# First three products of layer 0 of a two-layer attention model: advanced together over the arriving tiles of x

## The chip, the cores and the metric

The program runs on 1 core of one Trainium2 chip. The metric is device time in microseconds (us) of that core, given as the median of several runs of the whole program. The engines are PE (TensorE: matmuls and transposes), DVE (VectorE), ACT (ScalarE), POOL (GpSimd) and SP (SyncE, which here only issues DMAs). Each engine executes its instructions in the order of the program, and waits on semaphores for the others.

## The reference

The reference is a transformer of two layers over one sequence of 512 tokens of width 1024, in f32. Layer 0 mixes two kinds of attention heads. Eight "fox" heads have a decay from a forget gate. Eight "DSA" heads attend, per query, to the 128 keys that a small indexer scores highest, over a key-value latent of rank 128. Layer 1 has sixteen heads of block attention. Each layer ends with a gated feed-forward part with a short convolution. Cut to the part that the change touches:

```python
def rmsnorm(x, g):
    y = x * lax.rsqrt(jnp.mean(x * x, axis=-1, keepdims=True) + EPS) * g
...
    for layer in range(DEPTH):
        h = rmsnorm(x, attn_norm[layer])
        if layer % 2 == 0:
            proj = h @ w_in_even[i]
            fq, fk, fv, ff, dq, ckv, dkr, iq, ik, iw = jnp.split(proj, split_points, axis=-1)
            log_f = jax.nn.log_sigmoid(ff + b_fox_f[i])
            fox_out = fox_attention(fq, fk, fv, log_f)
            c_kv = rmsnorm(ckv, g_ckv[i])
            iq = apply_partial_rope(iq, cos, sin)
            ik = apply_partial_rope(ik, cos, sin)
            o_lat = dsa_attention(q_lat, q_rope, c_kv, k_rope, iq, ik, iw, dsa_topk)   # top 128 keys per query
            x = x + mixed @ w_out_even[i]
        else:
            ...
        x = x + conv_glu_ffn(rmsnorm(x, ffn_norm[layer]), ...)
    return rmsnorm(x, final_norm)
```

## The kernel before, in words

Everything is held transposed: x is eight tiles xT[0] to xT[7] of 128 features by 512 tokens. The factor 1/rms of a token does not depend on the feature, so the products start from x times g, and the factor is multiplied onto their results when they leave PSUM (RB, CR and SR hold it, spread over 128 partitions).

**Products.** An f32 product is made of three matmuls of a reduced-precision type. Each operand is split into a high part (a cast) and a low part (the rest): xh and xl of x, wh and wl of the weights. `mm3` adds high times high (line 154), high times low (155) and low times high (156). `proj` runs a product over the eight feature tiles: 24 matmuls of 512 columns, 5 to 6 us at full rate. `prep` makes xh on ACT (line 169) and xl on DVE (170) for one tile of x.

**Weights.** They come in chunks of 128 by 1024. `chunk` loads one by SP into a buffer "raw", ACT casts it to "wh", and DVE subtracts to get "wl"; once the flag lo_on_pool is set, from the fox heads' weights on, POOL subtracts instead (145 to 147). There are three buffers of each kind (N_W). SP goes through its loads in order, and a load waits until the raw buffer of three chunks ago is free.

**PSUM.** There are four pools of banks of 512 columns: "mm" with 3 for products, "S" with 2 for scores, "T" with 2 for transposes, "O" with 1 for the output of a head.

**The start, lines 479 to 552.** SP loads x tile 0, the first half of the chunk misc, x tile 1, the second half, the other x tiles, then iq0, iq1 and ckv whole. misc holds the small outputs (the indexer's key and weights, the rotary key, the forget gates), iq0 and iq1 the indexer's queries, ckv the latent. Product misc runs while x arrives. Squares of x go to ACT and are added into acc (the first three on POOL, 181) and acc2 (DVE, 499); DVE adds the two (500). `rope_angles` is a chain of tiny DVE operations for the rotary angles, and `rope_tables` transposes them on PE (tabT, 314). `rstd_main` then makes the factor 1/rms: PE transposes acc (st_n, 187), DVE sums it and takes the inverse root by Newton steps on four columns (194 to 196), PE transposes that back while spreading it (bc_n, 199), ACT copies it to RB. `rope` (217 to 221) takes a product from PSUM with CR and SR, one of its multiplications on POOL; `scaled` (226) takes one with RB.

**The heads, from line 585 on.** Eight head pairs of layer 0, four fox and four DSA, each with its key and query products (fk, fq), a value product (fv) for two pairs, the score blocks s_f in pool "S", their softmax (335 to 337), and the product with the values. `index_scores` (526) and `select` (543) are put between them by a work list: the indexer's scores go into tmask1 to tmask3, and sixteen rounds of MAX and MATCH_REPLACE on DVE find the top 128 per query; line 550 turns the result into a mask, which the first DSA head needs.

**What sets the order.** The code above only declares dependencies and an order of writing. A scheduler in the framework places the instructions of every engine into one fixed row per engine, by estimates of its own, and puts in the waits. So an edit at the start can move instructions on an engine far behind it.

## Time and profile before

| | before |
|---|---|
| median of 3 runs | 1278.89 us (1277.62 to 1280.02) |
| profiled execution, its own time | 1276.6 us |
| its span in the profile | 1274.8 us |
| granted clock of PE, mean | 0.994 of 2.4 GHz |
| PE busy | 1224.2 us, 96% |
| DVE busy | 845.7 us, 66% |
| ACT busy | 591.7 us, 46% |
| POOL busy | 311.0 us, 24% |

The times of single instructions below come from the profiled execution. A share of busy time is a mean over the whole span; stages differ. A busy PE counts a matmul from its start to its modelled end, and matmuls overlap.

### The profile page before, as it was taken

The numbers are of one execution on the slowest core, as the hardware profiler recorded it, in microseconds if no ns is written. First come the engines' busy times: TensorE is split into PE (matmuls) and PEld (weight loads), VectorE is DVE, ScalarE is ACT, GpSimd is POOL, SyncE is SP. The second block draws the span as 40 slices with busy tenths as digits, with TensorE's granted clock in tenths as the row PEclk, the third lists the DMA queues.
The fourth block names the chain that finished last, engine by engine and source line by source line (L and its number), as shares of the span: only waits on it lengthen the run. The fifth ranks groups of instructions, "written<-read, shape, count | busy, mean of one in ns | idle before, by whom it ended". The sixth has DMA issues, their size and how long they took to land.

```text
span 1274.8 us, 17004 instructions
## 1 busy us (share of the span) xinstructions
PE 1224.2 (96%) x6148; PEld 1024.0 (80%) x6148; DVE 845.7 (66%) x1629; ACT 591.7 (46%) x1011; POOL 311.0 (24%) x354
## 2 busy tenths in 40 slices
PE   6899989999999999999999999999999999999996
PEld 4778767778888888888888788778788888888896
DVE  7899998776555345554467879787755533665564
ACT  5585667654333123333336556556433321333443
POOL 3586656541110001110114323222111100111000
PEclk9999999999999999999999999999999999999998
DMA  5223222222333233333323232222233333223363
GB/s 191 67 77 106 76 59 73 61 73 93 99 99 99 92 91 99 99 100 99 100 90 93 85 97 68 82 83 67 83 100 99 99 99 98 88 97 99 118 189 107
DMA packets 37379, 120.95 MB, mean 95 GB/s; under 512 B 4736, under 2 KB 4864, under 8 KB 37296
## 3 DMA queue, kind: packets, MB, share of 16 engines
q1 hardware_dynamic: 36368, 118.51, 30.4%
q10 hardware_dynamic: 864, 1.17, 0.3%
q8 instruction: 48, 0.79, 0.3%
q14 instruction: 35, 0.29, 0.1%
q0 software_dynamic: 64, 0.20, 0.0%
HBM read 109.37 MB, written 2.10 MB: 87 GB/s over the span
## 4 chain that ended last, share of the span: by engine, by line
PE 79%; DVE 14%; ACT 3%; issue 3%; POOL 0%; DMA 0%; DVEq 0%; ACTq 0%; POOLq 0%
PE mm_d L155 6%; PE mm_d L154 6%; PE mm_d L156 6%; PE mm_u L156 6%; PE mm_u L155 6%; PE mm_u L154 6%; PE mm_g L155 6%; PE mm_g L154 6%; PE mm_g L156 6%; DVE tmask L548 1%; DVE xl L170 1%; PE o_m L367 1%; DVE m L547 1%; PE t_m L358 1%; PE o_m L368 1%
## 5 line engine op out<-in xcount | busy, mean ns | idle before, releaser
L422 POOL TENSOR_TENSOR cv<-cv,sg 128x512 f32<-128x512 f32 x44 | 56.9, 1293 | 543.0 <-ACT sg L421 543.0
L155 PE MATMUL mm_d<-a_l,wh_d 128*128 128x512 f32 (+1 forms) x440 | 152.7, 347 | 0.0
L156 PE MATMUL mm_d<-a_h,wl_d 128*128 128x512 f32 (+1 forms) x440 | 152.5, 347 | 0.0
L154 PE MATMUL mm_d<-a_h,wh_d 128*128 128x512 f32 (+1 forms) x440 | 152.5, 347 | 0.0
L155 PE MATMUL mm_g<-xl,wh_g 128*128 128x512 f32 x352 | 137.1, 390 | 0.0
L156 PE MATMUL mm_u<-xh,wl_u 128*128 128x512 f32 x352 | 137.1, 390 | 0.0
L154 PE MATMUL mm_g<-xh,wh_g 128*128 128x512 f32 x352 | 136.9, 389 | 0.0
L154 PE MATMUL mm_u<-xh,wh_u 128*128 128x512 f32 x352 | 136.9, 389 | 0.0
L155 PE MATMUL mm_u<-xl,wh_u 128*128 128x512 f32 x352 | 136.9, 389 | 0.0
L156 PE MATMUL mm_g<-xh,wl_g 128*128 128x512 f32 x352 | 136.9, 389 | 0.0
L143 ACT CAST wh_d<-raw_d 128x1024 fp32r<-128x1024 f32 x55 | 57.8, 1050 | 122.4 <-PE mm_d L155 83.5
L149 DVE TENSOR_TENSOR wl_d<-raw_d,wh_d 128x1024 fp32r<-128x1024 f32 x55 | 67.6, 1229 | 66.7 <-ACT wh_d L143 66.5
L143 ACT CAST wh_u<-raw_u 128x1024 fp32r<-128x1024 f32 x44 | 46.4, 1054 | 131.6 <-PE mm_g L155 114.6
L154 PEld LDWEIGHTS mm_d<-a_h,wh_d 128*128 128x128 f32 x440 | 83.3, 189 | 10.4
L156 PEld LDWEIGHTS mm_d<-a_h,wl_d 128*128 128x128 f32 x440 | 83.3, 189 | 10.3
L155 PEld LDWEIGHTS mm_d<-a_l,wh_d 128*128 128x128 f32 x440 | 83.3, 189 | 10.2
L417 DVE TENSOR_TENSOR gs<-mm_g,RB 128x512 f32<-128x512 f32 x44 | 30.4, 692 | 90.7 <-PE mm_g L156 90.2
L424 DVE TENSOR_TENSOR us<-mm_u,RB 128x512 f32<-128x512 f32 x44 | 30.4, 692 | 81.2 <-PE mm_u L156 81.2
L154 PEld LDWEIGHTS mm_g<-xh,wh_g 128*128 128x128 f32 x352 | 66.1, 188 | 13.8
L154 PEld LDWEIGHTS mm_u<-xh,wh_u 128*128 128x128 f32 x352 | 66.1, 188 | 13.8
L155 PEld LDWEIGHTS mm_u<-xl,wh_u 128*128 128x128 f32 x352 | 66.1, 188 | 13.7
L156 PEld LDWEIGHTS mm_g<-xh,wl_g 128*128 128x128 f32 x352 | 66.1, 188 | 13.6
(775 smaller groups left out, 3080.2 us busy)
## 6 DMA issues: line engine op xcount, KB each, us to landing
raw_d<-in_w SPq DMA_DIRECT2D x55, 512.0 KB, 3.5
raw_g<-in_w SPq DMA_DIRECT2D x44, 512.0 KB, 3.5
raw_u<-in_w SPq DMA_DIRECT2D x44, 512.0 KB, 3.5
raw_oe<-in_w SPq DMA_DIRECT2D x8, 512.0 KB, 3.5
raw_mv<-in_w SPq DMA_DIRECT2D x8, 512.0 KB, 3.6
raw_mk<-in_w SPq DMA_DIRECT2D x8, 512.0 KB, 3.6
raw_mq<-in_w SPq DMA_DIRECT2D x8, 512.0 KB, 3.6
raw_oo<-in_w SPq DMA_DIRECT2D x8, 512.0 KB, 3.5
```

The source lines that it names most:

```text
L143: A.copy(wh, raw)
L149: V.tensor_tensor(wl, raw, wh.bitcast(F32), op=OP.subtract)
L154: PE.matmul(out, ah, bh, start=first, stop=False)
L155: PE.matmul(out, ah, bl, start=False, stop=False)
L156: PE.matmul(out, al, bh, start=False, stop=last)
L170: V.scalar_tensor_tensor(xl[:, d], xT[:, d], gc, xh[:, d].bitcast(F32), op0=OP.mult, op1=OP.subtract)
L358: PE.transpose(t[:, n * P:n * P + P], probs[i][:, j * P:j * P + P], ident)
L367: PE.matmul(o[:, o0:o0 + w], vj, ph[:, c0:c0 + w], start=j == 0, stop=False)
L368: PE.matmul(o[:, o0:o0 + w], vj, pl[:, c0:c0 + w], start=False, stop=j == NB - 1)
L417: V.tensor_tensor(gs, og, RB, op=OP.mult)
L422: G.tensor_tensor(cv, cv, sg, op=OP.mult)
L424: V.tensor_tensor(us, ou, RB, op=OP.mult)
```

## The change

`chunk` loses its form with a cut, and `proj` the form that takes weights already loaded. A new function, `first_products`, takes the three chunks misc, iq0 and iq1, and an order of arrivals. Each step loads one x tile and preps it, or loads one half of a chunk (512 columns) and splits it on ACT and DVE. After every step it writes all the matmuls of the three products that have become possible: those of the x tiles so far against the halves so far. The three results stand in PSUM pools "O" (misc) and "S" (iq0, iq1) where they stood in "mm". The square of an x tile is written right behind its step, and `rope_angles` behind the fourth x tile.

Product ckv is now written right after the three, ahead of the last sum into acc, `rope_tables` and `rstd_main`; it stood behind the rotary work on misc and iq. The copy into cmask is written after the three products.

```diff
--- before.py
+++ after.py
@@ -128,17 +128,13 @@
 
     lo_on_pool = False
 
-    def chunk(name, cut=0):
-        raw = wp.tile([P, 1024], F32, tag="raw", bufs=N_W, name=f"raw_{name}")
-        wh = wp.tile([P, 1024], F32R, tag="wh", bufs=N_W, name=f"wh_{name}")
-        wl = wp.tile([P, 1024], F32R, tag="wl", bufs=N_W, name=f"wl_{name}")
-        if cut:
-            for s in (slice(0, cut), slice(cut, 1024)):
-                nc.sync.dma_start(raw[:, s], w_d[idx[name]][:, s])
-                split(wh[:, s], wl[:, s], raw[:, s])
-                if s.start == 0:
-                    nc.sync.dma_start(xT[:, 1], xT_d[:, 1])
-            return wh, wl
+    def w_tiles(name):
+        return (wp.tile([P, 1024], F32, tag="raw", bufs=N_W, name=f"raw_{name}"),
+                wp.tile([P, 1024], F32R, tag="wh", bufs=N_W, name=f"wh_{name}"),
+                wp.tile([P, 1024], F32R, tag="wl", bufs=N_W, name=f"wl_{name}"))
+
+    def chunk(name):
+        raw, wh, wl = w_tiles(name)
         nc.sync.dma_start(raw, w_d[idx[name]])
         A.copy(wh, raw)
         if lo_on_pool:
@@ -155,8 +151,8 @@
         PE.matmul(out, ah, bl, start=False, stop=False)
         PE.matmul(out, al, bh, start=False, stop=last)
 
-    def proj(name, w=None):
-        wh, wl = w or chunk(name)
+    def proj(name):
+        wh, wl = chunk(name)
         o = ps("mm", f"mm_{name}")
         for k in range(KT):
             s = slice(k * P, k * P + P)
@@ -477,19 +473,11 @@
 
 
     acc = sq_acc(0)
-    nc.sync.dma_start(xT[:, 0], xT_d[:, 0])
-    w = chunk("misc", 512)
-    for d in range(2, KT):
-        nc.sync.dma_start(xT[:, d], xT_d[:, d])
     nc.gpsimd.dma_start(const, const_d)
-    G.tensor_copy(cmask[:, 384:], const[:, C_TRI:C_TRI + P])
-    cs = rope_angles()
-    for d in range(KT):
-        prep(d, 0, None)
-    pmisc = proj("misc", w)
-    w = [chunk("iq0")]
     acc2 = tmp("acc2")
-    for d in range(KT):
+    angles = []
+
+    def first_square(d):
         if d < 4:
             square(d, acc)
         else:
@@ -497,12 +485,46 @@
             A.activation(s, xT[:, d], AF.Square)
             if d > 4:
                 V.tensor_tensor(acc2, acc2, s, op=OP.add)
+
+    def first_products(names, order):
+
+        w = {n: w_tiles(n) for n in names}
+        o = {n: ps(tag, f"mm_{n}") for n, tag in names.items()}
+        done = {n: 0 for n in names}
+        xs, halves_of = 0, {n: 0 for n in names}
+        for what in order:
+            if what == "x":
+                nc.sync.dma_start(xT[:, xs], xT_d[:, xs])
+                prep(xs, 0, None)
+                xs += 1
+            else:
+                h = halves_of[what]
+                s = slice(512 * h, 512 * h + 512)
+                raw, wh, wl = w[what]
+                nc.sync.dma_start(raw[:, s], w_d[idx[what]][:, s])
+                split(wh[:, s], wl[:, s], raw[:, s])
+                halves_of[what] += 1
+            for n in names:
+                while done[n] < min(xs, 4 * halves_of[n]):
+                    k = done[n]
+                    s = slice(k * P, k * P + P)
+                    mm3(o[n], w[n][1][:, s], w[n][2][:, s], xh[:, k], xl[:, k], k == 0, k == KT - 1)
+                    done[n] += 1
+            if what == "x":
+                first_square(xs - 1)
+                if xs == 4:
+                    angles.append(rope_angles())
+        return [o[n] for n in names]
+
+    pmisc, *piq = first_products({"misc": "O", "iq0": "S", "iq1": "S"}, [
+        "x", "misc", "x", "iq0", "x", "iq1", "x", "x", "misc", "x", "iq0", "x", "iq1", "x"])
+    G.tensor_copy(cmask[:, 384:], const[:, C_TRI:C_TRI + P])
+    pckv = proj("ckv")
     V.tensor_tensor(acc, acc, acc2, op=OP.add)
-    w.append(chunk("iq1"))
     V.tensor_copy(selr[0:96, :P], const[0:96, C_SEL:C_SEL + P])
     V.tensor_copy(selr[96:128, :P], const[64:96, C_SEL:C_SEL + P])
     V.tensor_scalar(selr[:, P:], const[:, C_FSEL:C_FSEL + 8], 0.5, None, op0=OP.mult)
-    rope_tables(cs)
+    rope_tables(angles[0])
     rcol = rstd_main(acc, "n0")
     rope_scaled()
 
@@ -520,7 +542,7 @@
     for b in range(NB):
         PE.transpose(t[:, b * P:b * P + P], ym[:, b * P:b * P + P], ident)
     A.activation(iwT, t.rearrange("p (b c) -> p b c", b=NB)[:, :, 104:108], AF.Copy, scale=0.0625)
-    iq = [stack_q(rope(proj(f"iq{h}", w[h]), f"iq{h}"), f"iq{h}") for h in range(2)]
+    iq = [stack_q(rope(piq[h], f"iq{h}"), f"iq{h}") for h in range(2)]
 
 
     def index_scores(i):
@@ -549,7 +571,7 @@
         if rounds.stop == TOPK // 8:
             V.tensor_scalar(sc, sc, -2e38, NEG, op0=OP.is_gt, op1=OP.mult)
 
-    y = scaled(proj("ckv"), "ckv")
+    y = scaled(pckv, "ckv")
     sq = tmp("sqkv")
     A.activation(sq, y, AF.Square)
     _, bc = rstd_of(sq, P, "kv")
```

What the scheduler makes of it is shown at three places. The numbers at the names' ends count tiles and differ between the two programs.

First PE, at the boundary of the first products: mm_misc and mm_iq are the results, xh and xl the parts of x, wh and wl those of the weights. Before, the last three matmuls of misc, and the first three of iq0:

```order
L154 MATMUL mm_misc<-xh,wh_misc 128x512
L155 MATMUL mm_misc<-xl,wh_misc 128x512
L156 MATMUL mm_misc<-xh,wl_misc 128x512
L154 MATMUL mm_iq_313<-xh,wh_iq_198 128x512
L155 MATMUL mm_iq_313<-xl,wh_iq_198 128x512
L156 MATMUL mm_iq_313<-xh,wl_iq_199 128x512
```

Now, nine matmuls on one tile of x, three for each product:

```order
L150 MATMUL mm_misc<-xh,wh_misc 128x512
L151 MATMUL mm_misc<-xl,wh_misc 128x512
L152 MATMUL mm_misc<-xh,wl_misc 128x512
L150 MATMUL mm_iq_113<-xh,wh_iq_107 128x512
L151 MATMUL mm_iq_113<-xl,wh_iq_107 128x512
L152 MATMUL mm_iq_113<-xh,wl_iq_108 128x512
L150 MATMUL mm_iq_114<-xh,wh_iq_110 128x512
L151 MATMUL mm_iq_114<-xl,wh_iq_110 128x512
L152 MATMUL mm_iq_114<-xh,wl_iq_111 128x512
```

The products of iq0 (mm_iq_113) and iq1 (mm_iq_114) stand among those of misc, where they stood behind all of them.

Next PE around st_n, the transposes of acc from which the norm's factor is made. Before, it stood within iq0's product:

```order
L314 MATMUL tabT<-const,exp_tab 128x128 x8
L154 MATMUL mm_iq_313<-xh,wh_iq_198 128x512
L187 MATMUL st_n_258<-const,acc_100 128x128 x4
L155 MATMUL mm_iq_313<-xl,wh_iq_198 128x512
L156 MATMUL mm_iq_313<-xh,wl_iq_199 128x512
L154 MATMUL mm_iq_350<-xh,wh_iq_226 128x512
```

Now, at the end of ckv's product and within that of fv, the first value product of the fox heads:

```order
L152 MATMUL mm_ckv<-xh,wl_ckv 128x512
L310 MATMUL tabT<-const,exp_tab 128x128 x5
L150 MATMUL mm_fv__0_483<-wh_fv_0_486,xh 128x256
L151 MATMUL mm_fv__0_483<-wl_fv_0_487,xh 128x256
L152 MATMUL mm_fv__0_483<-wh_fv_0_486,xl 128x256
L150 MATMUL mm_fv__0_483<-wh_fv_0_486,xh 128x256
L151 MATMUL mm_fv__0_483<-wl_fv_0_487,xh 128x256
L152 MATMUL mm_fv__0_483<-wh_fv_0_486,xl 128x256
L150 MATMUL mm_fv__1_484<-wh_fv_0_486,xh 128x256
L183 MATMUL st_n_345<-const,acc_100 128x128 x4
L151 MATMUL mm_fv__1_484<-wl_fv_0_487,xh 128x256
```

In PE's row st_n moved from behind 46 product matmuls to behind 72, the 24 of ckv and 7 of fv.

Last DVE, in the softmax of the second fox head: prt_f and mx_f are the numerator and maximum of a score block, sm_f a sum; the MAX and MATCH_REPLACE on tmask are a round of the selection. Before:

```order
L335 ISA prt_f_861,mx_f_0_866<-s_f_0_862,cmask 128x128
L335 ISA mx_f_0_866 128x1
L548 MATCH_REPLACE tmask_89<-m_1_1354,tmask_89 128x256
L335 ISA prt_f_861,mx_f_1_876<-s_f_1_872,cmask 128x256
L335 ISA mx_f_1_876 128x1
L547 MAX m_1_1357<-tmask_89 128x8
L337 RECIPROCAL sm_f_0_867<-sm_f_0_867 128x1
L548 MATCH_REPLACE tmask_89<-m_1_1357,tmask_89 128x256
L335 ISA prt_f_861,mx_f_2_886<-s_f_2_882,cmask 128x384
L335 ISA mx_f_2_886 128x1
L337 RECIPROCAL sm_f_1_877<-sm_f_1_877 128x1
L547 MAX m_1_1360<-tmask_89 128x8
```

Now:

```order
L331 ISA prt_f_867,mx_f_0_872<-s_f_0_868,cmask 128x128
L331 ISA mx_f_0_872 128x1
L569 MAX m_1_1351<-tmask_89 128x8
L331 ISA prt_f_867,mx_f_1_882<-s_f_1_878,cmask 128x256
L331 ISA mx_f_1_882 128x1
L333 RECIPROCAL sm_f_3_814<-sm_f_3_814 128x1
L333 RECIPROCAL sm_f_0_873<-sm_f_0_873 128x1
L570 MATCH_REPLACE tmask_89<-m_1_1351,tmask_89 128x256
L331 ISA prt_f_867,mx_f_2_892<-s_f_2_888,cmask 128x384
L331 ISA mx_f_2_892 128x1
L237 TENSOR_TENSOR fq_a<-sc_fq_942,fq_a 64x512
L333 RECIPROCAL sm_f_1_883<-sm_f_1_883 128x1
```

Fewer rounds stand between the blocks, and the query work of the second pair (fq_a) stands among them.

## Rows read from the trace of the kernel before

**Rows 1.** The page, first part: busy us, share of the span, instructions.

```profile
PE 1224.2 (96%) x6148; PEld 1024.0 (80%) x6148; DVE 845.7 (66%) x1629; ACT 591.7 (46%) x1011; POOL 311.0 (24%) x354
```

**Rows 2.** Windows: stretch, us, busy of PE PEld DVE ACT POOL, PEclk, DMA, GB/s.

```profile
60.00:200.00 140.00, 130.38 (x706) 106.34 (x704) 131.75 (x377) 93.83 (x209) 93.96 (x120) 1.00 0.27 74
67.00:184.00 117.00, 109.87 (x596) 89.76 (x596) 111.24 (x324) 76.58 (x168) 79.92 (x102) 1.00 0.29 81
...
220.00:280.00 60.00, 59.57 (x294) 48.19 (x294) 45.62 (x98) 36.59 (x77) 33.54 (x40) 1.00 0.25 71
```

**Rows 3.** Timeline of PE: start, us, line, out<-in, shape, count [idle before <-releaser].

```profile
14.60 0.79 PE L155 MATMUL mm_misc<-xl,wh_misc 128*128 128x512 f32 x1 [2.54 <-DVE xl L170]
...
19.45 0.39 PE L154 MATMUL mm_misc<-xh,wh_misc 128*128 128x512 f32 x1
19.68 0.40 PE L155 MATMUL mm_misc<-xl,wh_misc 128*128 128x512 f32 x1
...
25.59 1.03 PE L314 MATMUL tabT<-const,exp_tab 128*128 128x128 f32 x8
...
26.86 0.66 PE L187 MATMUL st_n<-const,acc 128*128 128x128 f32 x4
...
32.70 0.73 PE L199 MATMUL bc_n<-const,y_n 128*128 128x128 f32 x4 [2.20 <-DVE y_n L196]
...
33.66 0.63 PE L154 MATMUL mm_iq<-xh,wh_iq 128*128 128x512 f32 x1
34.08 0.63 PE L155 MATMUL mm_iq<-xl,wh_iq 128*128 128x512 f32 x1
...
37.71 0.39 PE L154 MATMUL mm_ckv<-xh,wh_ckv 128*128 128x512 f32 x1
...
43.76 0.28 PE L155 MATMUL mm_fv__0_477<-wl_fv,xh 128*128 128x256 f32 x1
43.88 0.28 PE L156 MATMUL mm_fv__0_477<-wh_fv,xl 128*128 128x256 f32 x1
```

**Rows 4.** DVE's waits from 60 to 210 us: total, times, longest.

```profile
DVE ry_dq L221 <- POOL rs_dq L220: 1.7, 2, 1.5
```

**Rows 5.** Timeline of PE, where the DSA heads' products begin.

```profile
203.07 0.50 PE L623 MATMUL mm_dk<-kr,selr 128*128 128x512 f32 x1 [1.48 <-DVE ry_dq L219]
```

**Rows 6.** Timeline of DVE: first and last of the selection's masks.

```profile
67.11 0.48 DVE L538 SCALAR_TENSOR_TENSOR tmask<-rl,iwT,cmask 128x256 f32<-128x256 f32 x1
...
177.07 0.67 DVE L547 MAX8 m<-tmask 128x8 f32<-128x512 f32 x1
...
180.77 0.73 DVE L550 TENSOR_SCALAR tmask<-tmask 128x512 f32<-128x512 f32 x1
```

**Rows 7.** Windows, during the first loads (columns as in rows 2).

```profile
4.00:12.00 8.00, 4.03 (x7) 1.88 (x7) 5.88 (x17) 6.74 (x12) 3.19 (x3) 1.00 1.03 376
```

**Rows 8.** Tiles, at the start: ns min/median/max, first and last start.

```profile
L169 ACT ACTIVATE xh<-xT,vec x8: 707/708/722, 5.3 to 12.7; 128x512 fp32r<-128x512 f32 x8
...
L170 DVE SCALAR_TENSOR_TENSOR xl<-xT,vec,xh x8: 740/742/751, 6.5 to 18.0; 128x512 fp32r<-128x512 f32 x8
...
L127 DVE TENSOR_TENSOR wl_misc<-raw_misc,wh_misc x2: 676/684/692, 7.8 to 11.9; 128x512 fp32r<-128x512 f32 x2
```

**Rows 9.** Timeline of DVE at the start, around acc.

```profile
8.38 1.25 DVE L270 TENSOR_SCALAR ang_n<-ang_r 128x32 f32<-128x32 f32 x1
...
24.09 0.69 DVE L500 TENSOR_TENSOR acc<-acc,acc 128x512 f32<-128x512 f32 x1
```

**Rows 10.** Timeline of DVE, beside POOL's split of weights and away from it.

```profile
29.10 0.61 DVE L195 TENSOR_TENSOR h_n<-h_n,ms_n 128x4 f32<-128x4 f32 x1
...
32.00 0.16 DVE L194 SCALAR_TENSOR_TENSOR h_n<-y_n 128x4 f32<-128x4 f32 x1
...
36.85 1.77 DVE L221 TENSOR_TENSOR ry_misc<-ry_misc,rs_misc 128x512 f32<-128x512 f32 x1 [0.21 <-POOL rs_misc L220]
...
46.92 0.69 DVE L221 TENSOR_TENSOR ry_iq<-ry_iq,rs_iq 128x512 f32<-128x512 f32 x1
```

## The prediction, made before the changed kernel ran

> **What bounds the kernel now.** The first line of the page says that PE is busy for 1224.2 of 1274.8 us [rows 1], but that is a sum over stages with different limits. The change sits in the first 45 us, so I read that stage and the one that it feeds. Between 60 and 200 us, the attention heads of layer 0, DVE is busy for 131.75 of 140 us and PE for 130.38 [rows 2]. The two look equal. They are not: a 128x512 matmul at full rate shows 0.39 us of busy time, while the next one starts 0.23 us after it [rows 3], so short gaps on PE are hidden under the tail of the matmul before, and DVE's operations leave no such tail. The waits say the same. DVE's longest cause of waiting in this stage is 1.7 us in all, for a product of POOL [rows 4]. PE, at 203.07 us, stands 1.48 us until DVE has emptied a PSUM tile [rows 5]. After that PE has little idle time: 59.57 of 60 us are busy from 220 to 280 us [rows 2]. So what the start of the kernel is worth is read at DVE: DVE sets when PE comes through at about 203 us, and from there on the time is PE's.
>
> DVE in this stage does two things: the work of the heads, and the rounds of the top-128 selection (MAX and MATCH_REPLACE on tmask1 to tmask3), which fill its gaps. The last mask is done at 180.77 us [rows 6], and the first DSA head needs it. Rounds that are put off must be made up before that point.
>
> **The loads.** SP issues fourteen loads of 256 KB at the start (eight of x, six half chunks), where it issued ten of 256 KB and two of 512. The bytes are the same, and nothing else is queued on SP until a buffer of weights comes free. From 4 to 12 us the queues moved 376 GB/s [rows 7], and nearly all that was on its way was loads of 256 KB. The last x tile now has the 1.05 MB of iq0 and iq1 ahead of it: 2.8 us at that rate. DVE, as shown next, comes to it at about 22 us, some 7 us after it lands. Price nothing; 2.8 us on the last nine matmuls if that cover were gone.
>
> **The splits.** ACT makes the eight xh from 5.3 us on, 0.71 us each [rows 8]; with eight squares and six half casts that is 22 operations, about 0.6 us each with their overlap: some 13 us, to about 18. DVE is later. Its last xl began at 18.0 us and took 0.74 [rows 8]. The new order puts four half splits (0.68 us each [rows 8], some 0.6 apart), two sums of squares like them and four tiny operations ahead of that one, so it ends at about 22.8. Each of POOL's three additions to acc holds DVE for a good microsecond, as before: an operation on 32 columns that met one lasted 1.25 us [rows 9]. The last sum for acc began at 24.09 us [rows 9], and comes at about the same time now.
>
> **The products on PE.** Before, PE waited for the third x tile's xl and went on at 14.60 us with 7 matmuls done; it ran at the lower rate (0.43 us apart, as at 33.66) until 19.0 and at 0.23 us from then [rows 3]. In the new order that same xl falls at the same place of DVE's row, so the new PE also stands at 14.6 us, with 13 done and 59 to go, and DVE stays ahead of it from there. If the clock rises at 19.0 again, 10 of them run slowly and the 72 end at 30.1 us; if the denser work before 14.6 lets it rise at once, 59 x 0.228 = 13.5 us, 28.1. I take 29.1. Before, they ended where ckv begins, at 37.71 us [rows 3]. That is what the change gains on PE: 8.6 us.
>
> **What it does to the chain of the norm.** The scale of layer 0 comes from acc by four transposes (st_n), a chain of tiny DVE operations, and four more (bc_n), and PE executes in order. Before, st_n stood behind 46 product matmuls and ran at 26.86 us, bc_n at 32.70 [rows 3]. Now the scheduler has it behind all 72, the 24 of ckv and 7 of fv. The walk: 29.1; 24 x 0.228 = 5.5; 0.8 for the eight tabT transposes (1.03 with their tail [rows 3]); 0.5 taken for the wait until ckv's weights are split, which can start only when misc's buffer is free; 7 x 0.12 [rows 3] = 0.8. So st_n runs at 36.7, 9.8 us later, though acc lies ready since 25. The chain then takes 5.84 us as before, if POOL's split of weights runs beside it again: bc_n at 42.5. Without POOL it is 1.9 us shorter: four operations of the chain lasted over 0.6 us beside POOL's split, the like of them 0.16 behind it [rows 10]. With this and the early clock bc_n comes 6.9 us later, with the late clock 10.8.
>
> At bc_n DVE has done the same instructions in both orders, and 9.8 us more have gone by. PE in that time has done 37 matmuls of 512 columns and 31 of 256 more than before: 12.1 us of work.
>
> **From bc_n to the first mask.** Before, this took from 32.70 [rows 3] to 67.11 us [rows 6]: 34.4 us. In it, eight operations that read two SBUF tiles lasted 1.00 to 1.77 us where they ran beside POOL, against 0.69 alone (the first, and one alone, in [rows 10]): 4.5 us too long in all. Of the POOL pieces beside them, two chunks (wl_fv's second and wl_fk) now run while DVE waits for st_n, but wl_fq and the second pair's wl_fk take their place. I take half of the 4.5 us as saved, 2.2, with 0 and 4.5 as ends.
>
> The Trainium skill has a rule for this: "SBUF — State Buffer", section "Who interferes with whom", says that a DVE instruction with two SBUF inputs and a GpSimd instruction that reads SBUF exclude each other for the whole instruction. By that rule, if each of these operations met POOL again the sum would be 2.2 us longer, and if none did 2.3 us shorter. The trace agrees with it here, 1.77 against 0.69 us.
>
> There are new waits off that path: fk's first matmul waits for the copy of ckv out of PSUM, since misc and iq no longer use that pool and ckv and fv fill it, and fk and all behind it on PE wait with it; on ACT the cast for the second pair's fq stands ahead of the log-decay and waits until fk's product has let go of its buffer. Both come late because bc_n does, and I price them within the half that isn't saved. DVE is then 9.8 - 2.2 = 7.6 us late at the first mask; the ends are 6.9 - 4.5 = 2.4 and 10.8.
>
> **From the mask to 203 us.** The new order also runs more of the second pair's fk and fq ahead of the first softmax (36 more matmuls, 8.2 us), and DVE's row puts selection rounds off: at the third head nine fewer are done, until the seventh about eight fewer, at the first DSA head none. A round of 512 columns is a MAX of 0.67 us [rows 6] and a MATCH_REPLACE about as long, some 1.35 us, so 10.8 us of debt is paid between about 160 and 184 us. Over the whole stretch DVE's work is the same, and only its idle time can give something back. From 67 to 184 us that is 117.0 - 111.24 = 5.8 us [rows 2], much of it slivers between dependent instructions. I take half, 2.9, with 0 and 5.8 as ends.
>
> **The sum.** 9.8 - 2.2 - 2.9 = 4.7 us later at 203 us, and PE passes that on. The profiled execution took 1276.6 us (span 1274.8), so it would take 1281.3. The median lies 2.3 above it, at 1278.89, and I predict 1283.6. The ends: 2.4 - 5.8, or 3.4 faster, 1275.5; and 10.8 slower, 1289.7.
>
> **The rivals.** First, PE's lead is kept: it is 8.2 us of products ahead at the first softmax, and if DVE meets POOL nowhere and gives back all its idle time, the end is 1275.5. For it speaks that PE is nearly as busy as DVE; against it that DVE is 94% full between 60 and 200 us, and that PE's lead buys nothing where each score block waits for DVE. It decides once DVE is late at the first mask by less than it recovers, 5.8 us at most. Chance 0.13. Second, the two cancel: bc_n some 7 us late, most of the stretching by POOL gone, half of the idle time back: 0 to 2.5 us slower, 1280. Chance 0.24. Third, worse than the forecast: PE stands ahead of bc_n for over 2 us and falls to the lower clock, as it did behind its wait of 2.20 us at 32.70 (matmuls of 0.63 us) [rows 3], and the heads, with few rounds between their blocks, leave DVE idle while ACT and POOL finish: 1289 and more. Chance 0.15. That the three products don't advance together is no case of its own: their order is fixed, and only the clock moves their end.
>
> **How the numbers follow.** The forecast (2.6 to 9 us slower) has 0.48. Faster by over 0.2% (about what a measurement of this kernel can tell from no change, 2.6 us) has 0.13, within it 0.24, slower 0.48 + 0.15 = 0.63. The range leaves out most of the first rival and the far end of the third: 1276.3 to 1288.8.
>
> **What would show it.** The last of the 72 matmuls at 28 to 30 us; st_n at about 36.7 and bc_n near 42.5, with DVE idle ahead of st_n for some 6 us; the first tmask operation at 70 to 78 us; the last mask and the wait at mm_dk 3 to 9 us later than 180.77 and 203.07; from 220 us on the two traces shifted by a constant. I am wrong if st_n runs before 33 us, if the first mask comes before 70 us, or if DVE shows clear idle time between 80 and 180 us while PE has none.

## The result, and the profile of the changed kernel

The changed kernel takes 1287.95 us, median of 4 runs (1286.87 to 1290.65), the kernel before in the same runs 1278.33. The ratio is 1.0079, with a 95% interval from 1.0065 to 1.0092: 8.3 to 11.8 us slower, 9.6 by the medians. The profiled execution has a span of 1285.5 us, 10.7 more than that of before. That of before lies 1.7 us under its own median, so shifts between traces read a little too large.

The first line of its page hardly differs from [rows 1]; the loss isn't visible there:

```profile
PE 1229.9 (96%) x6148; PEld 1028.6 (80%) x6148; DVE 843.4 (66%) x1631; ACT 591.8 (46%) x1013; POOL 308.9 (24%) x354
```

The timeline of PE (start, us, line, tile) at the end of the first products; this answers to [rows 3]:

```profile
28.51 0.39 PE L152 MATMUL mm_iq<-xh,wl_iq 128*128 128x512 f32 x1
...
36.48 0.66 PE L183 MATMUL st_n<-const,acc 128*128 128x128 f32 x4
...
40.99 0.62 PE L195 MATMUL bc_n<-const,y_n 128*128 128x128 f32 x4 [0.97 <-DVE y_n L192]
```

The 72nd matmul of the first products starts at 28.51 us, so ckv begins at 28.73, 9.0 us earlier than in [rows 3]. But st_n comes 9.6 us later than before and bc_n 8.3. The timeline of DVE shows who pays (in brackets: idle time ahead, and what ended it); it answers to [rows 6, 10]:

```profile
27.58 0.01 DVE L214 LOAD_MASK_SELECT rs_misc<-mm_misc  x1 [2.76 <-PE mm_misc L152]
...
37.18 0.69 DVE L185 TENSOR_REDUCE ms_n<-st_n 128x4 f32<-128x512 f32 x1 [7.48 <-PE st_n L183]
...
45.05 1.21 DVE L217 TENSOR_TENSOR ry_misc<-ry_misc,rs_misc 128x512 f32<-128x512 f32 x1 [0.20 <-POOL rs_misc L216]
...
47.43 1.23 DVE L535 TENSOR_TENSOR ik_l<-ry_misc,ik_h 64x512 fp32r<-64x512 f32 x1
...
50.98 1.65 DVE L217 TENSOR_TENSOR ry_iq<-ry_iq,rs_iq 128x512 f32<-128x512 f32 x1
...
75.58 0.49 DVE L560 SCALAR_TENSOR_TENSOR tmask<-rl,iwT,cmask 128x256 f32<-128x256 f32 x1
...
194.83 0.42 DVE L572 TENSOR_SCALAR tmask<-tmask 128x512 f32<-128x512 f32 x1
```

DVE stands for 2.76 and 7.48 us with nothing to do. From there on it is late: the first mask at 75.58 us (before 67.11), the last at 194.83 (before 180.77). The windows up to the first mask, before and changed (columns as in rows 2), put it in one number:

```profile
0.00:67.11 67.11, 49.83 (x247) 40.43 (x247) 54.35 (x120) 37.12 (x57) 29.33 (x40) 0.97 0.38 125
```

```profile
0.00:75.58 75.58, 60.12 (x295) 49.66 (x296) 53.02 (x123) 39.46 (x61) 34.90 (x48) 0.98 0.38 124
```

DVE does 54.35 us of work in the one and 53.02 in the other; its idle time is 12.76 and 22.56 us. PE has 10.3 us of busy time more behind it, at a point that comes 8.5 us later. What becomes of that is seen at the fourth head, at the first two DSA heads (a head begins with a prt operation of 128 columns), and at the first sum into xT, which stands among the last DSA heads. Timeline of DVE, changed:

```profile
122.47 0.27 DVE L331 CUSTOM_DVE_ANT_0 prt_f<-s_f,cmask 128x128 f32<-128x128 f32 x1
...
183.09 0.27 DVE L331 CUSTOM_DVE_ANT_0 prt_d<-s_d,cmask 128x128 f32<-128x128 f32 x1
...
192.16 0.69 DVE L569 MAX8 m<-tmask 128x8 f32<-128x512 f32 x1
...
196.57 0.28 DVE L331 CUSTOM_DVE_ANT_0 prt_d<-s_d,cmask 128x128 f32<-128x128 f32 x1
...
232.62 0.68 DVE L399 TENSOR_TENSOR xT<-xT,mm_oe__0_2640 128x512 f32<-128x512 f32 x1
```

and before:

```profile
122.49 0.28 DVE L335 CUSTOM_DVE_ANT_0 prt_f<-s_f,cmask 128x128 f32<-128x128 f32 x1
...
179.11 0.68 DVE L547 MAX8 m<-tmask 128x8 f32<-128x512 f32 x1
...
180.56 0.28 DVE L335 CUSTOM_DVE_ANT_0 prt_d<-s_d,cmask 128x128 f32<-128x128 f32 x1
...
187.81 0.28 DVE L335 CUSTOM_DVE_ANT_0 prt_d<-s_d,cmask 128x128 f32<-128x128 f32 x1
...
223.08 0.67 DVE L403 TENSOR_TENSOR xT<-xT,mm_oe__0_2634 128x512 f32<-128x512 f32 x1
```

The fourth head begins at the same time in both: PE's lead has paid for the late factor. But nine selection rounds that stood ahead of it now stand behind it. They come due ahead of the last mask. The first DSA head begins 2.5 us late and the second 8.8: four MAX operations of the selection stand between the two, the last at 192.16 us, where before the last one ran at 179.11, ahead of both. At the first sum into xT the kernel is 9.5 us late. The rest of the 10.7 comes at st_n of layer 0's second norm. Timeline of PE, changed:

```profile
295.56 0.64 PE L183 MATMUL st_n<-const,acc 128*128 128x128 f32 x4 [2.27 <-DVE acc L177]
...
296.42 0.63 PE L152 MATMUL mm_g<-xh,wl_g 128*128 128x512 f32 x1
```

and before:

```profile
286.04 0.63 PE L187 MATMUL st_n<-const,acc 128*128 128x128 f32 x4 [2.28 <-DVE acc L181]
...
286.74 0.39 PE L156 MATMUL mm_g<-xh,wl_g 128*128 128x512 f32 x1
```

The same wait, 2.27 and 2.28 us; only in the changed kernel do the matmuls behind it take 0.63 us, at the lower clock: the granted clock is 0.50 of 2.4 GHz from 297 to 298 us, and 1.00 from 285.9 to 288 in the kernel before. That costs 1.1 us.

### The profile page after: what moved, and what is told of

It reads as the page before. It is cut to its first block, busy times and chain, and to the rows that moved or that the text cites. A ratio compares the mean times of both kernels' runs of the same rounds, so it can differ in the third digit from the quotient of the medians.

```text
span 1285.5 us, 17006 instructions
## 1 busy us (share of the span) xinstructions
PE 1229.9 (96%) x6148; PEld 1028.6 (80%) x6148; DVE 843.4 (66%) x1631; ACT 591.8 (46%) x1013; POOL 308.9 (24%) x354
## 4 chain that ended last, share of the span: by engine, by line
PE 78%; DVE 13%; ACT 3%; issue 3%; POOL 2%; DMA 0%; DVEq 0%; ACTq 0%; POOLq 0%
PE mm_d L152 6%; PE mm_u L152 6%; PE mm_d L151 6%; PE mm_d L150 6%; PE mm_u L151 6%; PE mm_u L150 6%; PE mm_g L152 6%; PE mm_g L151 6%; PE mm_g L150 6%; DVE tmask L570 1%; PE o_m L363 1%; DVE xl L166 1%; PE t_m L354 1%; DVE m L569 1%; PE o_m L364 1%
## 5 line engine op out<-in xcount | busy, mean ns | idle before, releaser
L150 PEld LDWEIGHTS mm_d<-a_h,wh_d 128*128 128x128 f32 x440 | 83.3, 189 | 10.3
L152 PEld LDWEIGHTS mm_d<-a_h,wl_d 128*128 128x128 f32 x440 | 83.3, 189 | 10.2
L151 PEld LDWEIGHTS mm_g<-xl,wh_g 128*128 128x128 f32 x352 | 66.4, 189 | 13.8
```

What stands on the lines that cost most here:

```text
L150: PE.matmul(out, ah, bh, start=first, stop=False)
L151: PE.matmul(out, ah, bl, start=False, stop=False)
L152: PE.matmul(out, al, bh, start=False, stop=last)
```

## The experiments

Four theories were on the table. Theory 1, the prediction's: the late norm factor makes DVE late, and DVE can't give it back. Theory 2: the loss is made in the heads, by selection rounds that the scheduler puts off. Theory 3: the half loads and the interleaving cost time themselves. Theory 4 came after the first runs: between bc_n and the first mask DVE is held by other engines, POOL above all, whatever bc_n does. The table has the start of bc_n, of the first tmask operation and of the first sum into xT by each trace, and the ratio to the kernel before.

| kernel | bc_n | first mask | first xT | ratio | 95% interval |
|---|---|---|---|---|---|
| before | 32.70 | 67.11 | 223.08 | | |
| changed | 40.99 | 75.58 | 232.62 | 1.0079 | 1.0065 to 1.0092 |
| 1 norm first | 28.96 | 68.67 | 227.65 | 1.0022 | 1.0013 to 1.0032 |
| 2 slow chain | 42.88 | 76.04 | 232.00 | 1.0074 | 1.0059 to 1.0089 |
| 3 ckv back | 35.71 | 71.06 | 231.24 | 1.0049 | 1.0032 to 1.0066 |
| 4 old pools | 35.68 | 70.33 | 226.91 | 1.0040 | 1.0024 to 1.0056 |
| 5 before, norm first | 31.60 | 67.70 | 225.67 | 1.0012 | 1.0003 to 1.0022 |
| 6 before, ckv up | 35.23 | 74.05 | 229.64 | 1.0047 | 1.0029 to 1.0064 |
| 7 before, few rounds | 32.11 | 66.51 | 222.75 | 0.9997 | 0.9986 to 1.0008 |
| 8 changed, few rounds | 40.03 | 75.04 | 222.17 | 1.0000 | 0.9990 to 1.0011 |
| 9 norm first, POOL's row | 28.49 | 69.20 | 230.40 | 1.0063 | 1.0049 to 1.0076 |
| 10 whole iq loads | 43.15 | 78.13 | 236.47 | 1.0091 | 1.0077 to 1.0106 |
| 11 changed, splits on DVE | 41.26 | 77.42 | 234.60 | 1.0089 | 1.0073 to 1.0104 |
| 12 norm first, splits on DVE | 29.30 | 69.09 | 227.43 | 1.0023 | 1.0014 to 1.0032 |

The starts are from one execution each. From the first mask to the first sum the kernel before takes 156.0 us and the changed one 157.0: of its 9.5 us there, 8.5 are lost by the first mask. Runs 2, 4, 6, 7 and 11 take 155.6 to 157.2 us for this stretch. Runs 1, 3, 5, 9, 10 and 12 take 158.0 to 161.2, so they lose 2 to 5 us more behind the first mask, and the start of the mask alone doesn't explain them.

**1. The norm first.** In the changed kernel:

```diff
-    V.tensor_tensor(acc, acc, acc2, op=OP.add)
+    with tc.high_priority():
+        rope_tables(angles[0])
+        V.tensor_tensor(acc, acc, acc2, op=OP.add)
+        rcol = rstd_main(acc, "n0")
+        rope_scaled()
...
-    rope_tables(angles[0])
-    rcol = rstd_main(acc, "n0")
-    rope_scaled()
```

> The changed kernel with the rotary tables, the last sum into acc, the factor of the norm and its tables CR and SR written ahead of ckv's product and given precedence over everything else. The three products still advance together, with the same loads. In PE's row st_n then stands within the last products (behind 50 of the 72 matmuls) instead of behind all of them, ckv and part of fv. Theory 1 (the loss is the late norm factor: whatever bc_n loses, DVE can't give back before 203 us): acc is ready at 24.3 us, st_n at about 25, the chain takes 4.5 us without POOL beside it, bc_n at about 29.8, which is 2.9 us earlier than before; the time comes out 2 to 4 us below the kernel before, 1274 to 1276.5. Theory 2 (the loss is made in the heads, by selection rounds that are put off and paid late): the rounds stand almost as before here (9, 12, 18, 32 at the first four heads, before 9, 13, 20, 33), so the time is that of before, 1278, within 1.5. Theory 3 (the half loads and the interleaving cost time themselves): 1283 or more.

It takes 1281.42 us: 6.8 of the 9.6 us are gone, so most of the loss is the norm's place, and theory 3 is out as the main cause. The time lies in none of the three ranges: bc_n is 3.7 us earlier than before and the first mask 1.6 later, so theory 1's gain didn't come. Timeline of DVE:

```profile
37.33 1.21 DVE L217 TENSOR_TENSOR ry_misc<-ry_misc,rs_misc 128x512 f32<-128x512 f32 x1 [2.76 <-POOL rs_misc L216]
...
68.67 0.48 DVE L561 SCALAR_TENSOR_TENSOR tmask<-rl,iwT,cmask 128x256 f32<-128x256 f32 x1
```

DVE waits 2.76 us for POOL, whose row has five pieces of fv's split ahead of misc's rotary multiplication.

**2. A slow chain in the kernel before.**

```diff
-        for _ in range(3):
+        for _ in range(17 if nm == "n0" else 3):
```

> The kernel before with fourteen more Newton steps in the norm factor of layer 0's attention, and nothing else: 42 operations on four columns between st_n and bc_n, about 0.197 us apart, 8.3 us. The selection rounds stand among the heads as before (10, 14, 20, 33 at the first four). Theory 1: bc_n at about 41, and all of the 8.3 us comes through: 1286 to 1288. Theory 2: DVE and PE have other work meanwhile and the heads' order isn't harmed: at most half comes through, 1278 to 1282.5. Theory 3 has nothing to say.

1287.80 us, 9.2 more than the kernel before and within theory 1's 1286 to 1288, with loads and heads' order as before. bc_n came 10.2 us later, not 8.3. Timeline of PE:

```profile
42.88 1.08 PE L199 MATMUL bc_n<-const,y_n 128*128 128x128 f32 x4 [9.56 <-DVE y_n L196]
...
46.57 0.80 PE L154 MATMUL mm_ckv<-xh,wh_ckv 128*128 128x512 f32 x1 [2.60 <-DVE ry_misc L219]
```

But PE stands still for the factor here, and ckv begins 8.9 us later than in [rows 3], as late as the first mask. The run shows that a late factor costs nearly all of its delay; since PE is as late as DVE in it, it doesn't show that the cost comes through DVE. In the changed kernel PE was early.

**3 and 4. ckv back at its old place, and the old PSUM pool.** Each in the changed kernel, third run:

```diff
-    pckv = proj("ckv")
...
-    y = scaled(pckv, "ckv")
+    y = scaled(proj("ckv"), "ckv")
```

> The changed kernel with ckv's product written at its old place, behind the rotary work; all else as changed. In PE's row st_n comes behind the 72 matmuls, the table transposes and 5 of ckv's, about 30.7 us; bc_n at about 35.2, 2.5 us later than before and 5.8 earlier than in the changed kernel. The selection rounds among the heads stand nearly as in the changed kernel (9, 14, 27, 31, 34 at heads two to six; changed 9, 11, 24, 27, 32; before 13, 20, 33, 36, 40). Theory 1: 2 to 3.5 us above the kernel before, 1280.5 to 1282. Theory 2: close to the changed kernel, 1285 to 1288. Theory 3: 1283 or more.

fourth run:

```diff
-    pmisc, *piq = first_products({"misc": "O", "iq0": "S", "iq1": "S"}, [
+    pmisc, *piq = first_products({"misc": "mm", "iq0": "mm", "iq1": "mm"}, [
```

> The changed kernel with the three first products in the PSUM pool of three banks that they had before, so that ckv's product can't begin until misc's result has been read, which needs the norm's factor. In PE's row st_n and bc_n then stand right behind the 72 matmuls and the table transposes, with nothing between the two; the selection rounds stand exactly as in the kernel before. st_n at about 29.8 us, bc_n at about 34.3, 1.6 later than before; PE stands still for some 4.5 us ahead of it and may run at the lower clock for a few us after. Theory 1: 1.5 to 3.5 us above the kernel before, 1280 to 1282. Theory 2: as before, 1278, within 1. Theory 3: 1283 or more.

bc_n is at 35.7 in both, 3.0 us late, and the first mask 4.0 and 3.2 us late. They take 1285.21 and 1282.98, more than theory 1 allowed; the third lies in theory 2's range, the fourth doesn't. The rounds stand among the heads nearly as in the changed kernel in the third and exactly as before in the fourth. From the first mask to the first sum the third takes 4.2 us longer than the kernel before, the fourth 0.6. So the places of the rounds may cost the third run some 3.6 us, though the PSUM pool differs too; by the medians the two are 2.2 us apart, with overlapping intervals. Theory 2 isn't shown by this, nor excluded for the third run. The changed kernel it doesn't carry: 8.5 of its 9.5 us are lost ahead of the first round.

**5 and 6. The kernel before with the norm first, and with ckv up.** Fifth run:

```diff
+    with tc.high_priority():
+        rope_tables(cs)
+        V.tensor_tensor(acc, acc, acc2, op=OP.add)
+        rcol = rstd_main(acc, "n0")
+        rope_scaled()
     w.append(chunk("iq1"))
```

> The kernel before, with the rotary tables, the last sum into acc, the norm's factor, CR and SR given precedence over everything else; the products one after the other and the loads as before. The sum into acc then stands ahead of iq1's split on DVE, st_n 8 rows earlier on PE; POOL's order (misc's rope behind the first split of fv) and the selection rounds stay as before. acc ready at about 23.7 us, bc_n at about 29.7, 3 us earlier. Theory 1, in the form that the first four runs left (what is passed on is how late the first mask is, and bc_n only through it): first mask at 64 to 65 us, time 2 to 3.5 us below the kernel before. Rival, theory 4 (DVE meets POOL or waits for it in the stretch up to the first mask whatever bc_n does, as the run with the norm first in the changed kernel did: bc_n 3.7 us earlier, first mask 1.6 us later): first mask at 66.5 us or later, time within 1 us of before or slower.

Sixth run:

```diff
+    pckv = proj("ckv")
     V.tensor_tensor(acc, acc, acc2, op=OP.add)
...
-    y = scaled(proj("ckv"), "ckv")
+    y = scaled(pckv, "ckv")
```

> The kernel before, with ckv's product alone written ahead of the last sum into acc, as the changed kernel has it; the three first products one after the other, in the old PSUM pool, with the old loads. In PE's row st_n moves from behind 46 product matmuls to behind 58 or so, 2.9 us; bc_n at about 35.5. POOL splits both halves of fv ahead of misc's rope. Selection rounds nearly as before (9, 12, 19, 33, 35, 39). Theory 1: first mask at 69.5 to 71 us, time 2.5 to 4.5 us above the kernel before. Theory 2 (the heads' order): within 1.5 of before.

The fifth missed: st_n ran at 24.73 us, but ckv's split (1.22 us) slipped into the chain, and four of its operations met POOL (0.65 us each), as four do before. So bc_n won 1.1 us instead of 3, and the first mask came 0.6 later; at 1280.01 us the run is 2.0 slower, more than this explains. The sixth took 1284.12, 6.1 us more than the kernel before and more than either theory had said. Timeline of PE:

```profile
35.23 0.62 PE L199 MATMUL bc_n<-const,y_n 128*128 128x128 f32 x4 [0.89 <-ACT wh_fv L143]
...
39.02 0.79 PE L154 MATMUL mm_iq<-xh,wh_iq 128*128 128x512 f32 x1 [3.17 <-DVE ry_misc L219]
...
46.45 0.39 PE L156 MATMUL mm_iq<-xh,wl_iq 128*128 128x512 f32 x1
```

bc_n is only 2.5 us late. But iq1's product now waits until DVE has read misc's result; before, it ended at 37.7 [rows 3], here it ends at 46.7, and the first mask is 6.9 us late. The first mask needs the factor and the products, and in this run the products are late.

**7 and 8. Few selection rounds.** 43 of the 48 rounds are left out, in both kernels:

```diff
-        for _ in rounds:
+        for _ in list(rounds)[:1]:
```

> The kernel before without 43 of the 48 selection rounds (one round is left in each group, so the mask of the DSA heads is wrong in content, not in shape): some 50 us less work for DVE between 67 and 181 us. Theory 1 (DVE sets the time up to 203 us, PE behind it is nearly full): PE becomes the bound of the stage, and of the 10 us that PE idles between 60 and 200 us a good part goes: 5 to 11 us below the kernel before, 1268 to 1274. If DVE is not the bound there, within 2 us of before. It is the base for the next run.

> The changed kernel without the same 43 of the 48 selection rounds. Against the kernel before with as few rounds: theory 1 says that the loss of 9.3 us was passed on by a DVE without slack, so that with slack PE's 8 us of products done early count instead: between 4 us faster and 3 us slower than that kernel. If the late factor costs PE itself (its clock, its own waits for the factor), the difference stays at 7 to 10 us.

This pair corrects the prediction's first paragraph. With 40 us of DVE's busy time gone, the kernel before takes 1277.41 us: nothing gained. So DVE isn't the bound of the heads alone; PE, with its waits for the other engines, needs the same time. The windows from 60 to 200 us, kernel before with few rounds:

```profile
60.00:200.00 140.00, 129.24 (x701) 107.03 (x700) 92.05 (x245) 92.44 (x206) 92.32 (x117) 0.99 0.27 76
```

Against [rows 2], DVE is busy for 92.05 instead of 131.75 us, PE as before. And the changed kernel with few rounds takes 1278.17, the same as that one: without the rounds the late factor costs nothing and PE's lead brings nothing. The two just cancel, at the fourth head already. Timeline of DVE, before and changed with few rounds:

```profile
123.61 0.29 DVE L335 CUSTOM_DVE_ANT_0 prt_f<-s_f,cmask 128x128 f32<-128x128 f32 x1 [0.21 <-PE t_f L358]
```

```profile
123.16 0.29 DVE L331 CUSTOM_DVE_ANT_0 prt_f<-s_f,cmask 128x128 f32<-128x128 f32 x1 [0.20 <-PE t_f L354]
```

So the loss needs the rounds: in the kernel before they just fit under PE's heads, in the changed one, where DVE comes to them late, they don't. Leaving them out takes away the late start of the rounds and their new places at once. That the late start weighs most is read from the changed kernel's trace, by the 8.5 us at the first mask.

**9. POOL's row.** The first experiment, with SR ahead of CR and precedence for the rotary work too:

```diff
-    ym = rope(pmisc, "misc")
+    with tc.high_priority():
+        ym = rope(pmisc, "misc")
...
+        iq = [stack_q(rope(piq[h], f"iq{h}"), f"iq{h}") for h in range(2)]
```

> The run with the norm first in the changed kernel (first of the experiments) once more, with SR made before CR and the rotary work on misc, iq0 and iq1 given precedence too, so that POOL has misc's rotary multiplication ahead of its first split of fv instead of behind five pieces of it. All else as there. In that run DVE stood 2.76 us for this multiplication. If POOL's row was what cost the first mask its lead (theory 1 with POOL as the late engine): that wait is gone, bc_n at 29 as there, first mask at 65 to 66.5 us instead of 68.67, and the time 2 to 3.5 us below that run, 1277.5 to 1279.5, about level with the kernel before. If the stretch up to the first mask is held by something else (DVE meets POOL's splits wherever they lie; theory 4): first mask at 68 or later, 1280.5 or more.

The wait for misc's multiplication is gone, and the run is slower than the first, 1285.65 us: 4.2 by the medians, 5.1 with each against the kernel before that ran beside it. ckv's split, 1.22 us in the first run, lasts 2.31 here beside that multiplication. Timelines of DVE, then of POOL:

```profile
31.61 2.31 DVE L145 TENSOR_TENSOR wl_ckv<-raw_ckv,wh_ckv 128x1024 fp32r<-128x1024 f32 x1
...
42.46 4.97 DVE L217 TENSOR_TENSOR ry_iq<-ry_iq,rs_iq 128x512 f32<-128x512 f32 x1 [1.19 <-POOL rs_iq L216]
...
69.20 0.48 DVE L562 SCALAR_TENSOR_TENSOR tmask<-rl,iwT,cmask 128x256 f32<-128x256 f32 x1
```

```profile
42.85 1.29 POOL L216 TENSOR_TENSOR rs_iq<-rs_iq,SR 128x512 f32<-128x512 f32 x1
44.10 2.78 POOL L143 TENSOR_TENSOR wl_fk<-raw_fk,wh_fk 128x256 fp32r<-128x256 f32 x4
```

An operation that takes 0.69 us alone [rows 10] lasted 4.97, until POOL's multiplication and its four pieces of fk's split were through. The first mask came at 69.20, half a microsecond after the first run's. It is 2.1 us later than in the kernel before, and the first sum 7.3; what costs the 5.2 us between isn't shown.

**10. Whole loads of iq0 and iq1.** In the changed kernel:

```diff
-                s = slice(512 * h, 512 * h + 512)
+                n = 1 if what == "misc" else 2
+                s = slice(512 * h, 512 * h + 512 * n)
...
-                halves_of[what] += 1
+                halves_of[what] += n
...
-        "x", "misc", "x", "iq0", "x", "iq1", "x", "x", "misc", "x", "iq0", "x", "iq1", "x"])
+        "x", "misc", "x", "iq0", "x", "iq1", "x", "x", "misc", "x", "x", "x"])
```

> The changed kernel with iq0 and iq1 loaded and split whole, 512 KB at the places of their first halves, misc still in halves. The prediction priced the half loads at nothing. The later x tiles then come about 1.4 us later each way, and DVE's splits of 1.23 us stand among the x splits. In PE's row the last of the 72 products stands where it stood, st_n some 10 rows later, behind more of fv. If the half loads matter little: the last product of the 72 at 28 to 31 us, st_n at 37 to 39, time within 2.5 us of the changed kernel, 1286 to 1290. If the halves carry the early products: last product after 33 us.

The last product starts at 30.69 us instead of 28.51, and the time is 1289.60, 1.7 over the changed kernel (2.3 with each against the kernel before that ran beside it) with overlapping intervals. The halves bring PE 2 us; a gain for the kernel isn't shown.

**11 and 12. Four splits on DVE.** In the changed kernel, and in the first experiment:

```diff
-        if lo_on_pool:
+        if lo_on_pool and name not in ("fv0_0", "fv0_1", "fk0", "fq0"):
```

> The changed kernel with the low parts of the first four chunks of the fox heads (both of fv, fk and fq of the first pair) made on DVE instead of POOL: four operations of 1.22 us more on DVE, sixteen pieces fewer on POOL. DVE's row has three of the four in the 7.5 us that it stands waiting for st_n, the fourth later. bc_n stays where it was, 41 to 42 us. Theory 4 (DVE's operations on two SBUF tiles are held up by POOL's splits, 4.4 us in all between bc_n and the first mask in the changed kernel, 2.9 of it beside these four chunks): first mask 1 to 2 us earlier than 75.58, and the time 1 to 2.5 us below the changed kernel, 1285.5 to 1287. If the overlap with POOL costs nothing by itself: first mask 1.2 us later, time 1288 to 1290.

> The first experiment (changed kernel, norm first) with the same four splits on DVE. There bc_n was at 28.96 us, but the first mask at 68.67: DVE stood 2.76 us for POOL's rotary multiplication behind five pieces of a split, and its operations were 5 us longer beside POOL. Here POOL is free for the rotary work, DVE does 4.9 us more. Theory 4: first mask at 65 to 66.5 us, time 2 to 4 us below that run, 1277.5 to 1279.5, about level with the kernel before. Against it: PE has to wait for fv's low part until about 47 us, 8 us later, and has no reserve either, as the runs with few selection rounds showed; then the time is 1281 or more although the first mask is early.

Neither gained: 1288.98 and 1281.52 us, the first mask 1.8 and 0.4 us later than without. In the eleventh DVE still met POOL's other work (ry_misc lasted 1.75 us, ik_l 1.69). In the twelfth POOL's busy time between bc_n and the first mask fell from 21.18 to 8.30 us and the first mask didn't come earlier; but the four splits add 4.9 us to DVE in that stretch. So moving POOL's work doesn't free the mask, and the runs don't price the meetings with POOL alone. In the twelfth the wait has also moved on. Timeline of ACT, then of DVE:

```profile
54.95 1.05 ACT L139 CAST wh_fq<-raw_fq 128x1024 fp32r<-128x1024 f32 x1 [7.70 <-PE mm_fv__1_484 L152]
...
61.01 0.63 ACT L592 ACTIVATE lu<-lu 32x512 f32<-32x512 f32 x1
```

```profile
61.67 0.69 DVE L593 TENSOR_TENSOR lm<-lm,lu 32x512 f32<-32x512 f32 x1 [2.03 <-ACT lu L592]
...
69.09 0.49 DVE L561 SCALAR_TENSOR_TENSOR tmask<-rl,iwT,cmask 128x256 f32<-128x256 f32 x1
```

ACT stands 7.70 us at the cast of fq's weights until PE has done with fv's, and the forget gate's exponential and logarithm are queued behind that cast; DVE's masks stand behind the logarithm. No run came out faster than the kernel before by more than its interval.

## Why the prediction was right, and where it was not

The median of 1287.95 lies in the range of 1276.3 to 1288.8, near its upper end; the forecast was slower by 4.7 us, the measured loss is about twice that.

- **Products and norm: right.** The 72 ended at 28.7 us (said 29.1), st_n ran at 36.48 (36.7). bc_n came at 40.99 (42.5): PE's matmuls came 0.23 us apart from 16.2 us on, where they were 0.43 apart until then, and one operation of the chain met POOL, not four. The bounds, 6.9 to 10.8 us late, hold the 8.3.
- **From bc_n to the first mask: the term that was mis-sized.** Half of the 4.5 us of stretching was to be saved. The stretch took 34.6 us where it was 34.4. Seven operations on two SBUF tiles lasted 1.08 to 1.65 us, such as ry_misc at 1.21, ik_l at 1.23 and ry_iq at 1.65: 3.7 us too long in all, beside other chunks' splits. What that saved went into idle time of DVE, 5.92 us where it was 5.25. The Trainium skill's rule ("SBUF — State Buffer", "Who interferes with whom") is that such a DVE operation and a POOL operation that reads SBUF keep each other out. The 4.97 us of the ninth run agrees with it, and of the prediction's cases the one that each operation met POOL again came nearest. The new wait of fk's first matmul for ckv's copy out of PSUM was there, 3.02 us at 53.88 on PE, with a granted clock of 0.66 from 53 to 58 us; it falls into the same stretch.
- **From the mask to 203 us: mis-sized too.** Half of DVE's 5.8 us of idle time (67 to 184 us) was to be given back. None was: over the same work, taken a little further, DVE's windows show 8.87 us of idle time before and 10.67 now:

```profile
67.11:205.82 138.71, 128.81 (x694) 105.05 (x695) 129.84 (x375) 93.00 (x207) 93.55 (x120) 0.99 0.29 79
```

```profile
75.58:215.00 139.42, 123.90 (x658) 100.10 (x656) 128.75 (x374) 90.68 (x204) 89.04 (x115) 0.96 0.27 72
```

With 8.3 us at bc_n and nothing given back the sum would have come to within 1.3 us of the 9.6. PE's mean granted clock also fell here, from 0.99 to 0.96; no run tells what that costs. The last mask was to be 3 to 9 us later and is 14.1. The prediction had no round left over at the first DSA head; four MAX operations stood behind its first block, and work of that head came ahead of the mask.
- **The total: in range partly by luck.** Two recoveries, 5.1 us together, didn't come, and bc_n came 1.5 us earlier than forecast. The range held because its far end allowed for almost no recovery, not because the sizes were right.
- **The bound: half right.** "DVE sets when PE comes through" fits the changed kernel, where a first mask 8.5 us late cost 9.6. The second run, 8.9 for 9.2, doesn't decide, as PE was late in it too. The sentence doesn't fit the seventh, where DVE's work fell by 40 us in this stretch and the time stayed. Both engines are near their limit here; what a loss on PE alone costs wasn't tried. The prediction's own row had it: PE's 130.38 beside DVE's 131.75 of 140 us [rows 2]; the argument that set PE's share aside didn't test whether PE's waits could shrink. Its first reason misread the rows besides: DVE's operations overlap too, as CR and SR of the kernel before, 0.69 us each, start at 34.09 and 34.70.
- **The rivals.** PE's lead was used up by the fourth head, against the late factor; with few rounds it makes the two kernels equal, not the changed one faster. The third rival's size was nearly met, but not by its mechanism at bc_n: PE stood 0.97 us there, and the granted clock was 1.00 from 40.9 to 46 us. DVE wasn't left idle among the heads either: from 100 to 180 us it was busy for 77.2 of 80.

What stays open is what it would take to make an early factor pay. Three versions had bc_n 3.4 to 4.2 us earlier than before, and their first mask was 1.6 to 2.1 us later. A wait on POOL, one on ACT, and DVE's meetings with POOL stand in the way in one or another of them; none was shown to hold the mask by itself, and an order that clears all of them at once wasn't tried. Open too is what these runs lose behind the first mask.

## What to carry to other kernels

An engine that runs ahead is worth only what the other engines can do with it: before moving a product up, look at which small operations it will stand in front of on an engine that executes in order, here four transposes that the whole norm hung on. Where a second engine is full, and part of its work has a deadline, count its idle time from the start: here waiting early became work that stuck out later, though the first engine had caught up by the fourth head. Where that work was left out, the waiting cost nothing. Price a recovery near zero unless a row shows idle time that is both large and in one piece; of the 5.1 us assumed here none came. And when an experiment delays one engine, look whether it delays the other too, as the slow chain did.

## What the runs showed of the hardware

A DVE operation on two SBUF tiles that takes 0.69 us alone lasted 4.97 us in the ninth run, beside five consecutive POOL operations on SBUF that by the trace all began after it: it can be held up by several in a row, not just by one. And a wait of the same length, 2.27 and 2.28 us at the same point of the program, was followed by the lower level of PE's clock, 0.50 of 2.4 GHz, in the changed kernel's execution and by full rate in that of the kernel before, a difference of 1.1 us.
